# A new order of steps for both mixing stages of a two-layer hybrid decoder, with its engine and buffer tables

## The chip, the core and the metric

The kernel runs on one core of a Trainium2 chip. The metric is the device time of one execution in microseconds (us). TensorE (PE) multiplies, VectorE (DVE), ScalarE (ACT) and GpSimd (POOL) work on tiles, SyncE (SP) issues the transfers. Each engine works through its own instructions in the order in which the program issued them, and waits where one needs a result that is not there.

## The reference, cut to what matters

Two layers, 512 tokens, width 1024, all float32. Each layer has a mixing stage and an MLP:

```python
for l in range(DEPTH):
    h = rms_norm(x, norm_mix_g[l])
    proj = h @ w_in[l]                     # 1024 -> 3328 columns
    p_att, p_conv, p_rwkv = jnp.split(proj, [3 * ATT_W, 3 * ATT_W + 3 * CONV_W], axis=-1)
    ...
    o_att = diff_attention(q, k, v, lam, subln_g[l], lambda_init)   # 6 heads, causal
    o_conv = short_conv(b_gate, c_gate, u, conv_w[l])
    o_rwkv = rwkv7_time_mix(p_rwkv, ...)                            # 6 heads, recurrent state
    mixed = jnp.concatenate([o_att, o_conv, o_rwkv], axis=-1)
    x = x + mixed @ w_out[l]
    h = rms_norm(x, norm_mlp_g[l])
    x = x + jnp.square(jax.nn.relu(h @ w_mlp_up[l])) @ w_mlp_down[l]
return rms_norm(x, final_norm_g)
```

## The kernel before

A float32 product is made of three passes on rounded operands: the weight's high part by the activation's high part, high by low, and low by high (`whi`, `wlo` and `ahi`, `alo`; in the trace `ahim`, `alom`). For this, each weight tile of 128 x 512 is loaded as `raw`, ScalarE casts it to `whi` (L687), and VectorE or GpSimd subtracts to get `wlo` (L699). The table `LO` says, by `x` or `y`, which of the two engines does each of a layer's subtractions; the nine of the three head groups of layer 0 stay on VectorE.

A mixing stage has 26 groups of the input projection (`pj`), each 24 passes of 128*128 by 512 columns into one PSUM buffer, then eight groups of the output projection (`po0_...`; the rows called `po` with `pT` are attention's product with the values), each in two cuts, and the first three groups of the MLP's up projection. Beside these run the three pairs of attention heads (letters A, B, C), the two halves of the convolution (U, V), and three pairs of rwkv heads (R, S, T), each with a triangular inverse (r, s, t). Attention's score product is `sc`, its transposed probabilities `ptt`. Rwkv works in chunks of 64 tokens: `pg`, `pbv`, `pa`, `pst` (the state step) and others are its products. An inverse ends in four products that each need the one before, through a copy or an addition: `px`, `py`, `pz`, `pzz`, then `pzw` uses it. Between `px` and `py` stand two copies on ScalarE (`rt`, L1194).

All of this is written as Python generators, each of which yields one step at a time. `drive` takes steps from them as the string `ORDER[l]` says: a letter is one generator, a number behind it says how many steps. So the string fixes the order of instructions on every engine. The letters for the projections and their weights are d (loads), w (casts), x and y (subtractions on VectorE and GpSimd), m (projection passes) and o (additions of the output); n, g, h, i, p, N, e, q and k are norms, rates, gates, inputs, constants.

Buffers that exist several times are taken by the table `SLOTS`: for each pool and tag a digit for each tile in turn. `ps/mm` has two PSUM buffers for the projections, `ps/rp` four for the small products, `ps/at` two for attention, `wp/raw`, `wp/whi` and `wp/wlo` three each for the weights. A tile that takes a buffer waits until the former tile in it has been read. Copy-outs from projection buffers are the rows with `vf`, `kf` (L1294, L1267), `pg` and `pk` (L812).

The MLP and everything else are not driven by these tables. There the kernel has 32 up groups and the down product `dn`, whose result is added to `x` in L1537.

Of the kernel before, what the change touches and what calls it, by code (L numbers as in the profile page):

```python
# [22 lines left out]
S = 512  # L23
# [3 lines left out]
C = 64  # L27
# [24 lines left out]
LO = ("xxyyxxxxyxxyxyxyxyxyyxxxxyyxyyxxxyxyxyyyxxyxyyxxxxxyxxyyyxxyxyyyxxyxxyxxyyx",  # L52
      "xyxyyxxxxxyxxxxxxxxxxyxxyyyyyyxxyxxxxyyyyyyyxxxxyxxyyxyxyyxxyyxyxyyxyxxxxx")

ORDER = (
# [1571 lines left out]
```

## Time and profile before

| what | value |
|---|---|
| median of three runs | 1265.12 us (1264.98 to 1265.78) |
| the profiled execution's own time | 1265.12 us |
| its span | 1263.3 us |
| mixing stage of layer 0 (0 to 292 us) | TensorE busy 283.65 us |
| MLP of layer 0 (292 to 633 us) | TensorE busy 338.47 us |
| mixing stage of layer 1 (633 to 913 us) | TensorE busy 276.81 us |
| MLP of layer 1 and the end (913 to 1263.3 us) | TensorE busy 341.70 us |
| TensorE's granted clock in the four | 1.00, 1.00, 1.00, 0.99 |

A row of the timeline has the start in us, the duration, engine, line, operation, output and inputs, the part of the TensorE array used (128*128 is all of it), the shape and the count, and in brackets the idle time before with what ended it. The rows of one TensorE stage overlap, because passes are pipelined: the distance of two starts tells what a pass cost, the duration does not. The file is 17 lines shorter after the change, so L290 is L273 there, L687 is L670, L699 is L682, and so on.

### The profile page before, as it was taken

What the parts mean: (1) busy time and instruction counts of PE and PEld (TensorE: products, weight loads), DVE (VectorE), ACT (ScalarE), POOL (GpSimd) and SP (SyncE); (2) the same over time, 40 slices, a digit from 0 to 9 for tenths busy, and PEclk for the clock granted to TensorE, in tenths of its full rate; (3) what the DMA queues carried; (4) which work ended last, traced back from release to release, by engine and by line L of the source; (5) the groups of instructions that cost most, each with busy time, mean ns of one, the idle gap of its engine ahead of it and who ended that gap; (6) DMA issues with size and microseconds to landing.
All of it is one profiled execution on the core that took longest, in us unless ns stands there. A gap on an engine that the chain in (4) does not pass through costs nothing.

```text
span 1263.3 us, 25161 instructions
## 1 busy us (share of the span) xinstructions
PE 1240.6 (98%) x9493; PEld 1049.3 (83%) x9493; DVE 913.4 (72%) x1894; ACT 697.7 (55%) x1479; POOL 335.5 (27%) x434
## 2 busy tenths in 40 slices
PE   9999999999999999999999999999999999999997
PEld 6777777787789898989878887887787989898987
DVE  6788888867976666765667787879598766666654
ACT  7675655646744544544475656564575545454553
POOL 1343526133300101010224345352431010111110
PEclk9999999999999999999999999999999999999999
DMA  6533333142343333321235334331434233333122
GB/s 212 159 85 94 109 94 101 52 133 84 100 126 101 101 101 100 101 84 51 75 103 146 98 102 110 98 97 60 133 93 133 92 109 95 107 99 102 59 75 76
DMA packets 84698, 127.93 MB, mean 101 GB/s; under 512 B 21472, under 2 KB 25568, under 8 KB 84576
## 3 DMA queue, kind: packets, MB, share of 16 engines
q1 hardware_dynamic: 83856, 125.77, 32.4%
q8 instruction: 75, 1.23, 0.4%
q10 hardware_dynamic: 720, 0.55, 0.1%
q14 instruction: 47, 0.39, 0.1%
HBM read 117.11 MB, written 9.18 MB: 100 GB/s over the span
## 4 chain that ended last, share of the span: by engine, by line
PE 71%; DVE 3%; ACT 1%; issue 1%; POOL 0%; POOLq 0%; DVEq 0%; ACTq 0%
PE dn L290 22%; PE pj L290 11%; PE pa L290 11%; PE pb L290 6%; PE up L290 6%; PE po L290 4%; PE dnF L290 3%; PE pc L290 3%; PE sc L290 1%; PE ptt L295 1%; PE pg L290 1%; DVE wlo L344 0%; DVE blo L1461 0%; DVE x L1537 0%; PE pyy L290 0%
## 5 line engine op out<-in xcount | busy, mean ns | idle before, releaser
L1405 POOL TENSOR_TENSOR ml<-m,mh 128x512 fp32r<-128x512 f32 x64 | 95.2, 1490 | 509.0 <-ACT mh L1404 490.8
L343 ACT CAST whi<-raw 128x512 fp32r<-128x512 f32 x142 | 88.0, 621 | 173.9 <-PE dn L290 158.2
L290 PE MATMUL dn<-mh,whi 128*128 128x512 f32 x448 | 175.4, 391 | 2.0 <-DVE x L1537 2.0
L290 PE MATMUL dn<-mh,wlo 128*128 128x512 f32 x448 | 174.7, 390 | 0.0
L290 PE MATMUL dn<-ml,whi 128*128 128x512 f32 x448 | 174.6, 390 | 0.0
L290 PE MATMUL pj<-ahim,whi 128*128 128x512 f32 x392 | 157.6, 402 | 4.4 <-DVE vf L1294 1.8
L290 PE MATMUL pj<-ahim,wlo 128*128 128x512 f32 x392 | 158.3, 404 | 0.0
L290 PE MATMUL pj<-alom,whi 128*128 128x512 f32 x392 | 158.2, 404 | 0.0
L687 ACT CAST whi<-raw 128x512 fp32r<-128x512 f32 x142 | 87.6, 618 | 93.3 <-PE pj L290 40.6
L699 POOL TENSOR_TENSOR wlo<-raw,whi 128x512 fp32r<-128x512 f32 x62 | 81.7, 1317 | 215.3 <-ACT whi L687 199.1
L1537 DVE TENSOR_TENSOR x<-dn,x 128x512 f32<-128x512 f32 x112 | 76.8, 686 | 76.7 <-PE dn L290 76.7
L344 DVE TENSOR_TENSOR wlo<-raw,whi 128x512 fp32r<-128x512 f32 x142 | 115.2, 811 | 11.3 <-ACT whi L343 10.7
L1476 DVE TENSOR_TENSOR slo_p<-s,shi_p 128x512 fp32r<-128x512 f32 x96 | 70.9, 741 | 63.5 <-ACT shi_p L1475 58.8
L290 PEld LDWEIGHTS dn<-mh,whi 128*128 128x128 f32 x448 | 84.1, 188 | 21.5 <-issue 2.4
L290 PEld LDWEIGHTS dn<-mh,wlo 128*128 128x128 f32 x448 | 84.1, 188 | 17.9
L290 PEld LDWEIGHTS dn<-ml,whi 128*128 128x128 f32 x448 | 84.1, 188 | 16.5
L290 PEld LDWEIGHTS pj<-ahim,whi 128*128 128x128 f32 x392 | 73.9, 188 | 19.9 <-issue 1.7
L1475 ACT CAST shi_p<-s 128x512 fp32r<-128x512 f32 x96 | 59.2, 617 | 49.7 <-PE pa L290 38.1
L290 PEld LDWEIGHTS pj<-ahim,wlo 128*128 128x128 f32 x392 | 73.8, 188 | 14.3 <-issue 0.9
L290 PEld LDWEIGHTS pj<-alom,whi 128*128 128x128 f32 x392 | 73.9, 188 | 14.0 <-issue 0.5
L290 PE MATMUL pa<-tlo,shi_p 128*128 128x256 f32 x288 | 81.4, 282 | 0.0
L290 PE MATMUL pa<-thi,shi_p 128*128 128x256 f32 x288 | 81.2, 282 | 0.0
(417 smaller groups left out, 3255.3 us busy)
## 6 DMA issues: line engine op xcount, KB each, us to landing
raw<-wts SPq DMA_DIRECT2D x389, 256.0 KB, 2.7
qs<-dqhi SPq DMA_DIRECT2D x24, 128.0 KB, 3.2
ks<-dkhi SPq DMA_DIRECT2D x24, 128.0 KB, 3.8
x<-xT SPq DMA_DIRECT2D x8, 256.0 KB, 4.5
dqhi<-qhi SPq DMA_DIRECT2D x6, 256.0 KB, 3.4
dqlo<-qlo SPq DMA_DIRECT2D x6, 256.0 KB, 3.0
dkhi<-khi SPq DMA_DIRECT2D x6, 256.0 KB, 2.7
dklo<-klo SPq DMA_DIRECT2D x6, 256.0 KB, 3.1
```

Of the source, the lines that this page charges most:

```text
L290: ins = nc.tensor.matmul(*a, **k)
L295: ins = nc.tensor.transpose(*a, **k)
L343: act.copy(hi[:, :n], raw[:, :n])
L344: (pool if a and lean[0] else dve).tensor_tensor(lo[:, :n], raw[:, :n], hi[:, :n].bitcast(F32), ALU.subtract)
L687: yield act.copy(hi[:, k0:k1], raw[:, k0:k1])
L699: yield eng.tensor_tensor(lo[:, k0:k1], raw[:, k0:k1], hi[:, k0:k1].bitcast(F32), ALU.subtract)
L1405: pool.tensor_tensor(lo, m, hi.bitcast(F32), ALU.subtract)
L1475: act.copy(hi, src)
L1476: dve.tensor_tensor(lo, src, hi.bitcast(F32), ALU.subtract)
L1537: dve.tensor_tensor(x[j], pt, x[j], ALU.add)
```

## The change

Only three tables change: `LO`, `ORDER` and the entries of `SLOTS` that follow from the order. No function and no operation is added or removed, apart from what follows from the order (table loads on ScalarE, waits). In the diff's core a line or two of each:

```diff
-LO = ("xxyyxxxxyxxyxyxyxyxyyxxxxyyxyyxxxyxyxyyyxxyxyyxxxxxyxxyyyxxyxyyyxxyxxyxxyyx",
-      "xyxyyxxxxxyxxxxxxxxxxyxxyyyyyyxxyxxxxyyyyyyyxxxxyxxyyxyxyyxxyyxyxyyxyxxxxx")
+LO = ("xxxxxxyyyxyyyyxxyyyyxxxxyyxyyyyxxxxxyyyyyyyxyxxyyxyyxyyyyxyyxyxyyxxyxxxxyy",
+      "xyyxxyyyyyxyxyxyxyxyxxyyyyyxyyxxxxxxyyyyyyyyyxxxxxxyyyyyyyyyyyxyyxxxxxxxyx")
...
-         "m A r m A m A m2 A h m2 w S m2 A2 x m S h A m S A d m2 r m2 r2 m r m w m r2 m3 A m2 y m2 A r A m d S m r m r A m h w m r S A y B m r S B r d "
+         "S r S2 r h r2 R r3 m7 x m3 r2 A r m5 r2 m3 d m A2 r m2 A S2 m w A2 r2 A3 r A3 y m2 R d r S d2 m4 w y m S m A2 m4 w m2 w S2 m2 r S r3 x r5 "
...
-         "ps/mm 01010100101010101010110101010101010101010101 "
+         "ps/mm 10101011010101010101001010101010101010101010 "
...
-         "wp/wlo 01201201201201201201201201201201201201201201201201201201201201201201201201 ")
+         "wp/wlo 21021021021021021021202102102102120120120120120120120120120120120120120120 ")
```

Of the 151 subtractions of the two mixing stages, 89 are on VectorE and 62 on GpSimd before, 67 and 84 after. ScalarE's table loads are 11 before and 17 after. TensorE has the same 7785 matmuls; 777 of its instructions wait on another engine before, 855 after.

Two places show what moves. The first is on TensorE, in layer 1, in the inverse of the first rwkv pair: `px` is the product whose copies `rt` the product `py` needs, `pj` are projection passes (of groups 16 and 11), `pbv` belongs to the same rwkv pair, `ptt` and `po` to attention. Before:

```order
L290 MATMUL px1_0_1_8745<-yi1_0_8733,ee1_0_8731 64x64 x2
L290 MATMUL pj1_16_8678<-ahim1_7_7869,wlo114_4_8648 128x512
L290 MATMUL pj1_11_8770<-ahim1_0_7799,whi109_0_8676 128x512
L290 MATMUL pj1_11_8770<-alom1_0_7800,whi109_0_8676 128x512
L295 MATMUL ptt1_0_0_3_8778<-cst_77,pp1_0_0_3_0_8702 128x128 x4
L290 MATMUL py1_0_0_8789<-x16_1_0_8715,rt1_0_8768 64x64 x2
...
L290 MATMUL po1_0_0_8808<-v1_0_8436,pT1_0_0_8578 64x64 x20
L290 MATMUL pj1_11_8770<-ahim1_0_7799,wlo109_0_8684 128x512
```

And at the same place after:

```order
L273 MATMUL px1_0_1_8738<-yi1_0_8724,ee1_0_8722 64x64 x2
L273 MATMUL pbv1_0_0_8759<-vt1_0_8349,kq1_0_8224 64x64 x2
L273 MATMUL pbv1_0_1_8760<-vt1_0_8349,kq1_0_8224 64x64 x2
...
L273 MATMUL py1_0_0_8781<-x16_1_0_8700,rt1_0_8755 64x64 x2
L273 MATMUL py1_0_1_8782<-xs1_0_8702,rt1_0_8755 64x64 x2
...
L278 MATMUL ptt1_0_0_3_8801<-cst_77,pp1_0_0_3_0_8679 128x128 x4
L273 MATMUL pj1_11_8711<-ahim1_3_7811,wlo109_0_8686 128x512
L273 MATMUL pj1_11_8711<-ahim1_4_7815,whi109_4_8715 128x512
```

Between `px` and `py` stood three projection passes and four transposes; now there are sixteen small passes of `pbv` on the same tile size (the two rows alternate four times), and the projection passes come behind `py` in one run.

The second place is on TensorE in layer 0, where projection group 25 takes the PSUM buffer of group 6, which is copied out to `vf`. `sc` is attention's score product, `pvt` a transpose, `pa` and `pg` are rwkv products. Before:

```order
L290 MATMUL pj0_6_585<-alom0_7_260,whi6_4_538 128x512
L290 MATMUL pj0_6_585<-ahim0_7_259,wlo6_4_550 128x512
L290 MATMUL pj0_25_638<-ahim0_0_128,whi25_0_583 128x512
L295 MATMUL pvt0_0_641<-cst_77,vf0_0_634 128x128 x4
L290 MATMUL pj0_25_638<-alom0_0_129,whi25_0_583 128x512
```

And after:

```order
L273 MATMUL pj0_6_555<-ahim0_7_282,wlo6_4_571 128x512
L273 MATMUL pa0_1_616<-za0_366,lx160_398 128x512
...
L278 MATMUL pvt0_0_631<-cst_77,vf0_0_628 128x128 x4
L273 MATMUL pg0_0_0_0_640<-ar0_0_611,bk0_0_612 64x128
...
L273 MATMUL sc0_0_0_0_1_688<-ks0_0_0_624,qs0_0_0_530 128x128
L273 MATMUL pj0_25_704<-ahim0_0_128,whi25_0_588 128x512
```

Group 25's first pass directly followed group 6's last; now sixteen rows of other products stand between them.

More of the change, by code (lines that the diff above doesn't have):

```diff
@@ L50 @@
 OWN = (0, 5)
-LO = ("xxyyxxxxyxxyxyxyxyxyyxxxxyyxyyxxxyxyxyyyxxyxyyxxxxxyxxyyyxxyxyyyxxyxxyxxyyx",
-      "xyxyyxxxxxyxxxxxxxxxxyxxyyyyyyxxyxxxxyyyyyyyxxxxyxxyyxyxyyxxyyxyxyyxyxxxxx")
+LO = ("xxxxxxyyyxyyyyxxyyyyxxxxyyxyyyyxxxxxyyyyyyyxyxxyyxyyxyyyyxyyxyxyyxxyxxxxyy",
+      "xyyxxyyyyyxyxyxyxyxyxxyyyyyxyyxxxxxxyyyyyyyyyxxxxxxyyyyyyyyyyyyxyyxxxxxxyx")
 ORDER = (
[57 rows of a table removed]
[40 rows of a table added]
 SLOTS = (
@@ L116 @@
          "cp/ro 010 "
-         "cp/rr 01 "
-         "cp/rst 01201201 "
-         "cp/rsx 01201201 "
-         "cp/ry 010 "
-         "cp/ys 010 "
-         "dp/dkhi 010 "
-         "dp/dklo 010 "
-         "dp/dm 010 "
-         "dp/dn 010 "
-         "dp/dqhi 010 "
-         "dp/dqlo 010 "
-         "mp/av 012 "
-         "mp/dc 010 "
-         "mp/ks 101010 "
-         "mp/lw 012 "
-         "mp/mix 01201210 "
-         "mp/mx 012301230123012301230123012301230123012301230123 "
-         "mp/oss 010 "
-         "mp/pe1 01010010100 "
-         "mp/pp 011001100110011001100110011001100110011001100110 "
-         "mp/qs 101010 "
-         "mp/s0q 010 "
-         "mp/sm4 012301230123012301230123 "
-         "mp/ta 010101010 "
-         "mp/tc 010110 "
-         "mp/tp 01234510245234513512041025023524520013000341351302 "
-         "mp/tq 010101010101 "
-         "mp/ty 010101010 "
-         "ps/at 010101010101010101010101010101010101010101010101010101010101010101010101010101010101 "
-         "ps/mm 01011101010001010101010101010101010101010 "
-         "ps/rp 01233303103102310231023102310231023102021301230123012032121023102310202130123012301230123012013201313021032 "
-         "wp/raw 01201201201201201201201201201201201201201201201201201201201201201201201201 "
-         "wp/sq 010100001010101 "
-         "wp/whi 01201201201201201201201201201201201201201201201201201201201201201201 "
-         "wp/wlo 01201201201201201201201201201201201201201201201201201201201201201201 ",
-         "cp/rk 010 "
-         "cp/ro 010 "
-         "cp/rr 01 "
+         "cp/rr 10 "
          "cp/rst 01201201 "
@@ L168 @@
          "mp/lw 012 "
-         "mp/mix 01201021 "
+         "mp/mix 01201120 "
+         "mp/mx 012301230123012301230123012301230123012301230123 "
+         "mp/oss 010 "
+         "mp/pe1 01010010101 "
+         "mp/pp 011001100110011001100110011001100110011001100110 "
+         "mp/qs 010101 "
+         "mp/s0q 010 "
+         "mp/sm4 012301230123012301230123 "
+         "mp/ta 010101010 "
+         "mp/tc 010110 "
+         "mp/tp 01234510222245414132053021021254205131515431421452 "
+         "mp/tq 010101010101 "
+         "mp/ty 010101010 "
+         "ps/at 101010101010101010101010101010010101010101010101010101010110101010101010101010101010 "
+         "ps/mm 01011101010001010101010101010101010101010 "
+         "ps/rp 01233301203102302302031203201032103210102312031203210320132013012301212031023102312031203103103210303120132 "
+         "wp/raw 01201201201201201201201201201201201201201201201201201210210210210210210210 "
+         "wp/sq 101010110101010 "
+         "wp/whi 01201201201201201201201201201201201201201201201201201201201201201201 "
+         "wp/wlo 01201201201201201201201201201201201201201201201210210210210210210210 ",
+         "cp/rk 010 "
+         "cp/ro 010 "
+         "cp/rr 01 "
+         "cp/rst 01201210 "
+         "cp/rsx 01201210 "
+         "cp/ry 010 "
+         "cp/ys 010 "
+         "dp/dkhi 010 "
+         "dp/dklo 010 "
+         "dp/dm 010 "
+         "dp/dn 010 "
+         "dp/dqhi 010 "
+         "dp/dqlo 010 "
+         "mp/av 012 "
+         "mp/dc 010 "
+         "mp/ks 010101 "
+         "mp/lw 012 "
+         "mp/mix 01201020 "
          "mp/mx 012301230123012301230123012301230123012301230123 "
@@ L178 @@
          "mp/tc 010100 "
-         "mp/tp 01234510245235423143150241324125123504132413453420 "
+         "mp/tp 01234510245454535151403524152450451230415041021052 "
          "mp/tq 010101010101 "
@@ L182 @@
          "ps/at 010101010101010101010101010101010101010101010101010101010101010101010101010101010101 "
-         "ps/mm 01010100101010101010110101010101010101010101 "
-         "ps/rp 01230123012301230123012301231023102021301230123012301230123021032121302310231023013201320123012323102130 "
-         "wp/raw 01201201201201201201201201201201201201201201201201201201201201201201201201 "
-         "wp/sq 010101010 "
-         "wp/whi 01201201201201201201201201201201201201201201201201201201201201201201201201 "
-         "wp/wlo 01201201201201201201201201201201201201201201201201201201201201201201201201 ")
+         "ps/mm 10101011010101010101001010101010101010101010 "
+         "ps/rp 10321032103210321023102312301230123231021302130213021302130123012323102130213021321321012320132020312301 "
+         "wp/raw 12012012012012012101201201201210210210210210210210210210210210210210210210 "
+         "wp/sq 101010101 "
+         "wp/whi 21021021021021021021021021021021021021021021021021021021021021021021021021 "
+         "wp/wlo 21021021021021021202102102102120120120120120120120120120120120120120120120 ")
 NG = NG_IN + NG_OUT + NG_UP + NG_DN
```

96 rows, old and new, of the table ORDER are left out of this document.

## The prediction

> **What bounds the kernel now.** I read the page first, then the windows cut at the stage borders, then TensorE's waits, and last the timeline of TensorE at single places. The page's span, its first part and the first line of its chain of waits:
>
> ```profile
> span 1263.3 us, 25161 instructions
> PE 1240.6 (98%) x9493; PEld 1049.3 (83%) x9493; DVE 913.4 (72%) x1894; ACT 697.7 (55%) x1479; POOL 335.5 (27%) x434
> PE 71%; DVE 3%; ACT 1%; issue 1%; POOL 0%; POOLq 0%; DVEq 0%; ACTq 0%
> ```
>
> TensorE is busy for 98% of the span and idle for 1263.3 - 1240.6 = 22.7 us; no other engine comes to three quarters. So the reader should see two places where time can be had at all: those 22.7 us, and the way TensorE's own passes follow each other, since a "busy" matmul here includes what it loses at its start. The windows are the mixing stage of layer 0, its MLP, the mixing stage of layer 1, and its MLP with the end (columns: window, length, then busy time and count of PE, PEld, DVE, ACT, POOL, then granted clock, DMA share, GB/s):
>
> ```profile
> 0.00:292.00 292.00, 283.65 (x2740) 223.65 (x2740) 227.05 (x570) 178.10 (x417) 112.92 (x180) 1.00 0.38 114
> 292.00:633.00 341.00, 338.47 (x1964) 297.69 (x1964) 237.53 (x382) 174.06 (x326) 56.63 (x40) 1.00 0.30 94
> 633.00:913.00 280.00, 276.81 (x2731) 222.77 (x2730) 211.59 (x541) 166.44 (x396) 114.89 (x178) 1.00 0.35 105
> 913.00:1263.30 350.30, 341.70 (x2063) 305.22 (x2062) 237.23 (x405) 179.09 (x342) 51.06 (x36) 0.99 0.30 95
> ```
>
> The change touches the first and third window alone. Their idle time is 292.00 - 283.65 = 8.35 and 280.00 - 276.81 = 3.19 us: 11.5 us in all. A search that only removed waits could bring no more than that. Everything beyond must come from the spacing of passes, so I price that first.
>
> **Small tiles among the projections.** A projection pass (pj) is 128*128 with 512 columns. The rwkv and inverse steps are float32 passes on 64*64, 32*32 or 128*64 tiles. TensorE at such a place, in the timeline (start, duration):
>
> ```profile
> 159.45 0.40 PE L290 MATMUL pj<-ahim,wlo 128*128 128x512 f32 x1
> 159.69 0.39 PE L290 MATMUL pj<-ahim,whi 128*128 128x512 f32 x1
> 160.01 0.27 PE L290 MATMUL py<-x,rt 64*64 64x64 f32 x2
> ...
> 160.48 0.23 PE L290 MATMUL py<-xs,rt 64*64 64x64 f32 x2
> 160.63 0.50 PE L290 MATMUL pj<-alom,whi 128*128 128x512 f32 x1
> 160.97 0.40 PE L290 MATMUL pj<-ahim,wlo 128*128 128x512 f32 x1
> ...
> 713.23 0.23 PE L290 MATMUL py<-xs,rt 64*64 64x64 f32 x2
> 713.38 0.80 PE L290 MATMUL po<-v,pT 128*64 128x64 f32 x20
> ```
>
> Starts of projection passes lie 0.23 apart (the row after 159.45 says 0.24 by rounding). Going in takes 160.01 - 159.69 = 0.32, that is 0.09 more. Between py rows lie about 0.47 / 15 = 0.03; coming out takes 0.15, so 0.12 more, and the first pass after it 0.34, so 0.11 more: 0.23 together. Going from one small tile size to another (the last two rows) takes 0.15, where twenty po passes take 0.80, 0.04 each: 0.11 more.
>
> I counted the switches in the two orders (which the order gives exactly). Projections into small tiles: 57 before, 31 now. Small tiles back to the projections: 56, now 25. From small size to small size: 21, now 59. The sum is 26 x 0.09 + 31 x 0.23 - 38 x 0.11 = 2.3 + 7.1 - 4.2 = **5.3 us less**, all of it on TensorE's path, as nothing covers the pass that comes after a switch.
>
> [...] With one price for every change the three counts would be 134 and 115 and the gain smaller; that is a rival below.
>
> Two further shapes stay on the full tile. The state step of rwkv (pst):
>
> ```profile
> 111.41 0.48 PE L290 MATMUL pj<-ahim,whi 128*128 128x512 f32 x1
> 111.73 0.40 PE L290 MATMUL pj<-alom,whi 128*128 128x512 f32 x1
> 111.96 0.39 PE L290 MATMUL pj<-ahim,wlo 128*128 128x512 f32 x1
> 112.19 0.33 PE L290 MATMUL pst<-st,ad 128*128 128x64 f32 x2
> 112.33 0.48 PE L290 MATMUL pj<-ahim,whi 128*128 128x512 f32 x1
> ```
>
> It puts 0.14 between 112.19 and 112.33, and the pass after such a one starts 0.32 later (111.41 to 111.73): 0.14 + 0.32 - 0.23 = 0.23, of which its own work is part; I take half, 0.12. Returns of this kind fall from 35 to 23: 12 x 0.12 = **1.4 us less** (bounds 0 and 2.8). Attention scores on 96 rows (sc) between projections fall from 41 to 20. No row here has them alone; between nothing and 0.09, the cheapest entry above, I take 0.05: **1.0 us less** (bounds 0 and 1.9).
>
> **Accumulators that are not yet empty.** The projections use two PSUM buffers in turn; a group's first pass waits until the former group's result there has been copied out. TensorE's waits (total, times, longest), and one of them in the timeline:
>
> ```profile
> PE pj L290 <- DVE vf L1294: 1.8, 2, 0.9
> PE pj L290 <- DVE pg L812: 1.1, 1, 1.1
> PE pj L290 <- DVE pk L812: 0.7, 1, 0.7
> PE pj L290 <- DVE kf L1267: 0.4, 1, 0.4
> 53.14 0.39 PE L290 MATMUL pj<-ahim,wlo 128*128 128x512 f32 x1
> 54.41 0.47 PE L290 MATMUL pj<-ahim,whi 128*128 128x512 f32 x1 [0.88 <-DVE vf L1294]
> ```
>
> The second pass starts 1.27 after the first instead of 0.23. Four groups of before follow the former user of their buffer by 0.23 to 1.03 us of TensorE work (pj0_25 is the shortest). In the new order the shortest such distance inside the stages is 1.68 us, as other steps stand between; only layer 1's first group, pj1_24, has 0.23, behind the last down product. The four rows add to **4.0 us less** (bounds 2 and 4). For pj1_24 a copy-out is this row, and what may come back is the second:
>
> ```profile
> L1537 DVE TENSOR_TENSOR x<-dn,x 128x512 f32<-128x512 f32 x112 | 76.8, 686 | 76.7 <-PE dn L290 76.7
> PE pssm L290 <- DVE accm L455: 0.8, 1, 0.8
> ```
>
> It loses about 0.69 - 0.23 = 0.5; the later wait of pssm at that place then shrinks. I take **0.2 us more** (bounds -0.3 and 0.6).
>
> **The inverse's chain.** Six inverses have four steps each in which a product goes through a copy into the next product. In such a step the copies and TensorE looked like this before:
>
> ```profile
> 778.85 0.69 PE L290 MATMUL px<-yi,ee 64*64 64x64 f32 x32
> 779.48 0.50 PE L290 MATMUL pj<-ahim,whi 128*128 128x512 f32 x1
> 779.58 0.65 ACT L1194 COPY rt<-px 128x256 f32<-128x256 f32 x2 [0.23 <-PE px L290]
> 780.60 0.27 PE L290 MATMUL py<-x,rt 64*64 64x64 f32 x2
> ```
>
> The last px pass starts some 0.15 before 779.48, the copies end at 780.23: the step needs 0.9 us, and TensorE's projections covered 1.27. Before, these covers were 1.26 to 2.37 in all six. Now they are 0.25, 0.25, 0.63, 0.88, 1.43 and 1.49, since runs of small tiles stand together. The uncovered part is 0.65 + 0.65 + 0.27 + 0.02 = 1.6; the other three steps keep 0.78 to 5.12, which leaves some 0.4 open where the need is 0.9. So **2.0 us more** (bounds 0 and the slower rival below).
>
> Of the other waits I only know their number: 777 TensorE instructions waited on another engine, now 855. The 22.7 idle us over 777 are 0.03 each; 78 more give **2.3 us more** (bounds 0 and 4.6).
>
> **Work beside the path.** These rows are the low-part subtractions, a table load, the casts, and one vector operation beside a GpSimd operation (L407, at 628.25) and mostly without (L440):
>
> ```profile
> L699 POOL TENSOR_TENSOR wlo<-raw,whi 128x512 fp32r<-128x512 f32 x62 | 81.7, 1317 | 215.3 <-ACT whi L687 199.1 <-PE pj L290 7.7 <-DVE mlo L880 2.7
> L699 DVE TENSOR_TENSOR wlo<-raw,whi 128x512 fp32r<-128x512 f32 x80 | 56.3, 706 | 6.0 <-ACT whi L687 5.5
> L1333 ACT ACT_TABLE_LOAD x1 | 1.3, 1283 | 0.0
> L687 ACT CAST whi<-raw 128x512 fp32r<-128x512 f32 x142 | 87.6, 618 | 93.3 <-PE pj L290 40.6 <-PE po L290 24.8 <-issue 17.8
> L407 DVE SCALAR_TENSOR_TENSOR alom<-x,prm,ahim 128x512 fp32r<-128x512 f32 x6 | 7.4, 1240 | 4.5 <-ACT ahim L406 4.5
> L440 DVE SCALAR_TENSOR_TENSOR alom<-x,prm,ahim 128x512 fp32r<-128x512 f32 x10 | 7.3, 747 | 4.5 <-ACT ahim L439 4.5
> 627.74 1.29 POOL L400 TENSOR_TENSOR accm<-accm,sqm 128x512 f32<-128x512 f32 x1 [2.02 <-ACT sqm L394]
> 628.25 1.34 DVE L407 SCALAR_TENSOR_TENSOR alom<-x,prm,ahim 128x512 fp32r<-128x512 f32 x1 [0.78 <-ACT ahim L406]
> ```
>
> 22 subtractions go from VectorE to GpSimd: 22 x 0.706 = 15.5 us less on the one, 22 x 1.317 = 29.0 more on the other, whose two windows are 39% and 41% full. Table loads rise from 11 to 17: 6 x 1.283 = 7.7 us more on ScalarE, 61% full there. Weights wait two buffers ahead, so I set all this at nothing; the cover is the weight queue. If it is gone, a late subtraction costs 1.317 - 0.706 = 0.6 each, at most 13 us; a load that meets one of the chain's copies costs its 1.28, six of them 7.7.
>
> [...]
>
> **The sum.** -5.3 - 1.4 - 1.0 - 4.0 + 0.2 + 2.0 + 2.3 = -7.2 us. The profiled execution's own time is 1265.12 us, its span 1263.3 with 1.8 us around it, and it equals the median of the three runs. So 1265.1 - 7.2 = **1257.9 us**.
>
> **The rivals.** *One price for every switch.* A detour costs 0.09 + 0.23 = 0.32, or 0.16 for each of two switches; 134 to 115 switches would save 19 x 0.16 = 3.0, not 5.3, and the full-tile shapes nothing: -3.0 - 4.0 + 4.5 = -2.5, **1262.6 us**. For it: one mechanism. Against it: the 0.15 from py to po. Chance 0.15.
>
> [...] Each of the 22 GpSimd subtractions slows one vector operation beside it by 1.240 - 0.747 = 0.49: 10.8 of the 15.5 us are gone, evictions come no earlier, and the four waits stay somewhere: -5.3 - 2.4 + 4.5 + two of them more by 0.5 each = -2.2, **1262.9 us**, about the same. For it: the rows above. Against it: the waits came from distance in the order, not from a full VectorE. Chance 0.15.
>
> *Slower: the inverse's copies queue.* TensorE runs in order, so a step whose copy is late holds all projections behind it, and the copies stand on ScalarE among casts (0.62) and more table loads. With 24 steps each late by one cast, 0.62, plus the 1.6 uncovered: 16.5 in place of 2.0, so -7.2 + 14.5 = +7.3, **1272.4 us**. It decides from (7.2 + 2.0) / 24 = 0.38 us a step on. For it: six covers of px now below or near the need. Against it: the other steps have projections between. Chance 0.19; half as bad gives 1265.
>
> *The change does not do what it says.* The table loads rise by six in a search that counts them; should they lie on the path, 7.7 us cancel the gain: 1265.6, counted with the case of no change.
>
> The forecast has 0.48, and 0.03 is for a gain beyond the bounds. About 0.2%, 2.5 us, is what a measurement of this kernel can tell from no change. Faster by more than that: the forecast, the tail, and over half of the two middle cases, 0.67. The rest of these and of the mild late copies is within, 0.13; slower 0.20. The range goes from all bounds at their best, -5.3 - 2.8 - 1.9 - 4.0 - 0.3 = -14.3, about 1251, to the slower rival's middle, 1269.
>
> **What would show it.** In the changed kernel's windows PE busy should fall by some 5 us over the two mixing stages, the copy-out waits (vf, pg, pk, kf) should be gone from TensorE's waits, and py <- rt should appear among them with about 2 us. PE busy unchanged would make the switch prices wrong; py, pz and pzz with over 10 us of waits would make the slower rival right; waits of pj on wlo of L682 would show GpSimd short.

## The result, and the profile after

The changed kernel takes 1287.38 us (median of four runs, 1285.28 to 1288.8) against 1265.09 for the kernel before: a ratio of 1.0174, 95% interval 1.0156 to 1.0191. That is 22 us slower, where 7 us faster was forecast. The profiled execution has a span of 1285.7 us.

To see where the time went I cut both traces at the same five places of the program: the first plain projection pass with a `wlo` of its own, the first pass of `dn`, the first `pj` of layer 1, its first `dn`, and the end. So the stretch called a body, and layer 1's mixing stage too, reaches to the first `dn` and holds the first up groups of the MLP. The windows of before (window, length, then busy time and count of PE, PEld, DVE, ACT, POOL, then granted clock, DMA share, GB/s):

```profile
0.00:27.60 27.60, 24.64 (x101) 17.20 (x102) 18.13 (x43) 19.27 (x36) 2.68 (x8) 1.00 0.70 229
27.60:336.36 308.76, 301.87 (x2826) 240.56 (x2825) 246.60 (x594) 187.10 (x432) 122.97 (x182) 1.00 0.34 101
336.36:633.64 297.28, 295.93 (x1778) 263.62 (x1776) 200.34 (x315) 145.90 (x277) 43.91 (x32) 1.00 0.30 94
633.64:954.70 321.06, 318.19 (x2915) 257.00 (x2916) 249.10 (x607) 194.41 (x446) 126.23 (x184) 1.00 0.35 104
954.70:1263.30 308.60, 300.00 (x1877) 270.96 (x1875) 199.22 (x336) 151.01 (x292) 39.72 (x30) 0.99 0.30 94
```

And of the changed kernel:

```profile
0.00:44.73 44.73, 31.48 (x101) 22.12 (x102) 18.24 (x43) 19.58 (x36) 6.15 (x11) 0.81 0.47 148
44.73:351.70 306.97, 297.38 (x2827) 242.49 (x2825) 256.13 (x584) 190.75 (x440) 133.10 (x188) 1.00 0.34 101
351.70:648.18 296.48, 295.20 (x1778) 263.85 (x1776) 199.24 (x316) 144.89 (x274) 42.78 (x31) 1.00 0.30 93
648.18:975.52 327.34, 317.20 (x2916) 259.77 (x2916) 265.42 (x595) 192.75 (x447) 145.54 (x196) 0.99 0.34 103
975.52:1285.70 310.18, 300.90 (x1877) 271.41 (x1875) 199.16 (x337) 151.39 (x293) 39.76 (x30) 0.99 0.30 94
```

Three things are to be seen. The **opening** does the same 101 instructions of TensorE in 44.73 us instead of 27.60: 17.1 us, the bulk of the loss. The **body of layer 0** is 1.8 us shorter: TensorE is busy 4.5 us less, and idle 9.59 instead of 6.89. **Layer 1's mixing stage** is 6.3 us longer: busy 1.0 us less, but idle 10.14 instead of 2.87. So the spacing did improve; the waits grew by more. The end is 1.6 us longer and the MLP of layer 0 is 0.8 shorter.

In the opening TensorE waits, and is then slow. Here `pj` stands for passes of the three head groups, whose weights are `whi_s` and `wlo_s`; an input tile's two roundings `ahim` and `alom` are called its entry. The changed kernel's windows around its waits, and the first of these in the timeline:

```profile
8.00:12.30 4.30, 0.68 (x4) 0.21 (x2) 1.99 (x4) 3.43 (x6) 0.00 (x0) 1.00 0.11 40
12.30:16.30 4.00, 4.00 (x11) 3.13 (x12) 3.51 (x6) 0.96 (x3) 0.00 (x0) 0.57 0.64 197
...
33.50:40.40 6.90, 6.82 (x25) 6.11 (x26) 1.05 (x7) 0.26 (x2) 0.00 (x0) 0.52 0.11 37
12.28 0.50 PE L273 MATMUL pj<-ahim,wlo_s 128*128 128x512 f32 x1 [3.62 <-DVE wlo_s L682]
12.84 0.62 PE L273 MATMUL pj<-alom,whi_s 128*128 128x512 f32 x1
13.26 0.63 PE L273 MATMUL pj<-ahim,wlo_s 128*128 128x512 f32 x1
```

After 3.62 us of waiting the passes start 0.42 apart (12.84 to 13.26) instead of 0.23, until about 16.25, 3.4 us later; the mean granted clock of the window is 0.57. The other waits of the opening are these:

```profile
22.79 0.57 PE L273 MATMUL pj<-alom,whi_s 128*128 128x512 f32 x1 [2.22 <-DVE alom L423]
28.93 0.50 PE L273 MATMUL pj<-ahim,whi_s 128*128 128x512 f32 x1 [2.59 <-ACT ahim L422]
33.58 1.86 PE L273 MATMUL pssm<-ones,accm 128*128 128x1 f32 x8 [2.88 <-DVE accm L438]
```

Their causes stand on the other engines. VectorE, ScalarE, GpSimd and SyncE of the changed kernel:

```profile
9.90 0.75 DVE L423 SCALAR_TENSOR_TENSOR alom<-x,prm,ahim 128x512 fp32r<-128x512 f32 x1 [2.24 <-ACT ahim L422]
11.67 1.49 DVE L682 TENSOR_TENSOR wlo_s<-raw,whi_s 128x384 fp32r<-128x384 f32 x3
27.33 0.62 ACT L670 CAST whi<-raw 128x512 fp32r<-128x512 f32 x1 [6.27 <-DMA raw<-wts]
28.16 1.33 ACT L422 ACTIVATE ahim<-x,prm 128x512 fp32r<-128x512 f32 x2
12.29 1.30 SPq L630 DMA_DIRECT2D raw<-wts  x3
13.64 1.86 SPq L634 DMA_DIRECT2D x<-xT  x4
23.13 9.59 SPq L630 DMA_DIRECT2D raw<-wts  x5
30.59 1.78 POOL L682 TENSOR_TENSOR wlo<-raw,whi 128x512 fp32r<-128x512 f32 x1 [1.30 <-ACT whi L670]
31.24 1.68 DVE L423 SCALAR_TENSOR_TENSOR alom<-x,prm,ahim 128x512 fp32r<-128x512 f32 x1
```

And SyncE of the kernel before, at its second group of loads:

```profile
7.38 2.44 SPq L647 DMA_DIRECT2D raw<-wts  x3
```

The subtractions `wlo_s` of 128x384 stand on VectorE behind an entry (`alom`) that waits 2.24 us for its input; until they are done, their `raw` buffers are not free, and SyncE's next loads, at 7.38 before, go at 12.29 (that the one holds the other is tested below). Later ScalarE stands 6.27 us at a cast of a plain weight tile whose load SyncE issues only at 23.13, and the casts of the inputs (`ahim`) queue behind it. The last `alom` takes 1.68 us beside a GpSimd subtraction, where the one at 9.90 takes 0.75, so by these rows some 0.9 of the 2.88 us for the sum is a collision of these two engines and not a step in the wrong place.

In the bodies, TensorE's waits on attention's `pp` and `ot` and on the inverse grew. Of the changed kernel, by total, times and longest:

```profile
PE ptt L278 <- DVE pp L1322: 4.2, 7, 1.2
PE pot L278 <- DVE ot L1347: 2.3, 2, 1.5
PE px L273 <- DVE yi L1169: 2.1, 2, 1.3
PE px L273 <- DVE sm L1318: 1.4, 1, 1.4
```

The kernel before has only the first of these in its list:

```profile
PE ptt L295 <- DVE pp L1339: 2.8, 4, 0.9
```

One of the longest waits of layer 1, with VectorE, GpSimd and TensorE of the changed kernel in its neighbourhood:

```profile
723.18 2.84 DVE L1158 TENSOR_TENSOR xs<-xd,cst 64x256 f32<-64x256 f32 x2
726.05 0.71 DVE L1169 STREAM_TRANSPOSE yi<-x 128x512 f32<-128x512 f32 x1
722.56 1.75 POOL L1167 TENSOR_TENSOR ee<-nn,cst 128x512 f32<-128x512 f32 x1
724.43 2.72 POOL L682 TENSOR_TENSOR wlo<-raw,whi 128x512 fp32r<-128x512 f32 x2
726.91 0.70 PE L273 MATMUL px<-yi,ee 64*64 64x64 f32 x32 [1.37 <-DVE sm L1318]
```

The product px needs `yi`, which ends at 726.76; the profile names `sm`, the operation behind it. Ahead of `yi` two operations `xs`, also steps of the inverse, take 2.84 us; by the groups of lines such a one took 0.420 on average before (twelve of them) and 0.834 now, before and after in turn:

```profile
L1175 DVE TENSOR_TENSOR xs<-xd,cst 64x256 f32<-64x256 f32 x12 | 5.0, 420 | 0.3
```

```profile
L1158 DVE TENSOR_TENSOR xs<-xd,cst 64x256 f32<-64x256 f32 x12 | 10.0, 834 | 0.2
L682 POOL TENSOR_TENSOR wlo<-raw,whi 128x512 fp32r<-128x512 f32 x84 | 114.0, 1361 | 194.2 <-ACT whi L670 174.0 <-PE po L273 7.6 <-DVE rst L369 5.0
```

The 0.834 is a mean of two kinds: five of the twelve took 1.40 to 1.43 us, each beside a GpSimd operation, and seven took 0.42, none beside one. Each of the two above begins while a GpSimd operation runs and ends about 0.3 us after it: the first at 724.59, behind `ee`'s end at 724.30, the second at 726.02, behind the end of the first `wlo` at 725.74. I summed this over a mixing stage: what each VectorE operation took, less the shortest of its kind in the two traces. That excess is 22.6 us in layer 0 and 18.3 in layer 1 before, 32.9 and 38.8 after; the sums move by some us with the ends of the stretch, and all of the growth lies in operations that ran beside a GpSimd operation. So 15.5 us of subtractions left VectorE, and about 31 us of lengthening of its other operations came.

### The profile page after: what moved, and what is told of

It is laid out like the page before. It is cut to its first block, busy times and chain, and to the rows that moved or that the text cites. A ratio compares the mean times of both kernels' runs of the same rounds, so it can differ in the third digit from the quotient of the medians.

```text
span 1285.7 us, 25139 instructions
## 1 busy us (share of the span) xinstructions
PE 1242.2 (97%) x9493; PEld 1059.6 (82%) x9493; DVE 938.2 (73%) x1872; ACT 699.4 (54%) x1485; POOL 367.3 (29%) x456
## 4 chain that ended last, share of the span: by engine, by line
PE 77%; DVE 13%; ACT 3%; DMA 2%; issue 2%; POOL 1%; SPq 0%; POOLq 0%; DVEq 0%; ACTq 0%
PE dn L273 22%; PE pj L273 15%; PE pa L273 11%; PE po L273 7%; PE pb L273 5%; PE dnF L273 3%; PE up L273 3%; PE pc L273 3%; PE sc L273 1%; PE ptt L278 1%; DMA raw<-wts 1%; DVE wlo L327 1%; DMA x<-xT 1%; DVE sm L1320 1%; DVE xs L1158 1%
## 5 line engine op out<-in xcount | busy, mean ns | idle before, releaser
L682 POOL TENSOR_TENSOR wlo<-raw,whi 128x512 fp32r<-128x512 f32 x84 | 114.0, 1361 | 194.2 <-ACT whi L670 174.0
L273 PE MATMUL pj<-alom,whi 128*128 128x512 f32 x392 | 155.1, 396 | 0.0
```

Source lines behind the costliest of these rows:

```text
L273: ins = nc.tensor.matmul(*a, **k)
L682: yield eng.tensor_tensor(lo[:, k0:k1], raw[:, k0:k1], hi[:, k0:k1].bitcast(F32), ALU.subtract)
```

## The experiments

Each ratio is against runs of the kernel before on the same chip. Versions that ran on different chips are compared by their ratios, times 1265 us, and not by their medians. Line numbers differ from version to version.

**Three subtractions early.** In the changed order:

```diff
-m x2 m3 q e w3 e4 q3 x3 e q2 m2 q
+m x2 m3 q e w3 x3 e4 q3 e q2 m2 q
```

> The changed order with one edit: the three 128x384 subtractions of the head groups stand directly behind their casts, ahead of two entry steps and three squares, instead of behind them. Theory A (one late step starts the whole loss of the opening): TensorE's 3.6 us wait at the second head pass goes, SyncE's next weight loads start near 8 us instead of 12.3, the inputs x4 to x7 come 4 us earlier and the three later waits of 2.2, 2.6 and 2.9 us shrink to a third: 1271 to 1277 us. Rival B (each wait of the opening has its own place in the order): only the first wait and the slow passes behind it go, 3.6 + 1.6 = 5 us: about 1282 us.

Measured 1282.97 us (1.0148, 1.0127 to 1.0169): 3.3 us back, and in the traces the opening is 3.9 us shorter, ending at 40.85. The wait on `wlo_s` is gone, though 1.56 us on `alom` stands near its place. SyncE's loads go at 7.63 instead of 12.29, so these subtractions did hold them, but the later waits stay: 2.2 us on `alom`, 3.5 on `ahim`, 2.9 on the sum. Theory A falls, rival B stands: one late step did not make the rest.

**The same three late in the kernel before.** The segment `m q m2 w m x e m w e m x m w d m3 x d e m3 d2 e q m3` became:

```diff
+q w e w e w d d e d2 e q x3 m16
```

> The kernel before with one edit: the same three 128x384 subtractions moved late, behind two entry steps. Theory A: a wait of TensorE of about 3.6 us, a lower granted clock behind it, weight loads and inputs 4 us later: 1275 to 1282 us. Rival B: the wait and its slow passes alone, about 1270 us.

Measured 1268.58 us (1.0024, 1.0015 to 1.0033), 3.1 us more. TensorE's wait on `wlo_s` is 1.5 us there, and one on `ahim` 1.9; SyncE's loads go at 10.49 instead of 7.38, and the opening ends at 31.10, 3.5 later. So the step costs about 3 us in both orders. Rival B's 1270 us is near; theory A's far larger loss did not come, though its chain is there in small: later loads, and a wait on inputs behind them.

**Casts behind the entries.** On top of the first edit, casts of plain weight tiles (w) were moved on ScalarE. First one cast went behind three more entry casts and two squares, to the place where the second already stood; then both went behind all entries:

```diff
-d6 w d k4 e3 m e m5 k2 q2 w m4 e m3 k e2 m2 q m n2
+d7 k4 e3 m e m5 k2 q2 w2 m4 e m3 k e2 m2 q m n2
```

> As the run with the three subtractions early, and the cast of the first plain weight tile moved behind three entry casts and two squares on ScalarE. Theory F (that cast waits on ScalarE for a weight load which comes late, and holds the inputs' casts behind it): TensorE's waits on ahim (3.5 us) and on accm (2.9 us) go, with the slow passes behind them: 1283 - 7 = about 1276 us. Rival G (the inputs themselves or the squares' buffers are late): within 2 us of 1283 us.

```diff
-d7 k4 e3 m e m5 k2 q2 w2 m4 e m3 k e2 m2 q m n2
+d7 k4 e3 m e m5 k2 q2 m4 e m3 k e2 m2 q m w2 n2
```

> As the run with the casts moved behind three entries, but now both casts of plain weight tiles stand behind all eight entries and the squares. In that run TensorE waited 6.3 us for the sum of squares, whose last square came behind an entry that stood behind these casts on ScalarE, and the casts waited 2.1 us for a weight load. Theory F (the casts ahead of the entries): that wait falls to under 1.5 us and the passes behind it are no longer slow: 1281.7 - 6 = about 1276 us or less. Rival G (inputs and squares are late by themselves): the wait stays above 4 us, 1280 us or more.

The first measured 1281.74 us (1.0124, 1.011 to 1.0138), within 2 us of 1283 as rival G had it; by the ratios it is 3.0 less, with intervals that overlap. Its trace does not fit rival G, and so the second was run: 1275.2 us (1.0083, 1.0065 to 1.0102), by the ratios another 5.2 us less, as theory F had it; the opening ends at 34.44 instead of 38.91. TensorE's wait for the norm's sum of squares, with the casts half way:

```profile
27.60 1.87 PE L167 MATMUL pssm<-ones,accm 128*128 128x1 f32 x8 [6.32 <-DVE accm L332]
```

And with them last:

```profile
23.48 1.86 PE L167 MATMUL pssm<-ones,accm 128*128 128x1 f32 x8 [2.23 <-DVE accm L332]
```

Half way, the waits had only moved from the inputs to the sum, since the last entry, and behind it VectorE's last addition to the sum (`accm`), still came after the casts. With the casts last, 2.2 us are left where theory F had said under 1.5.

**The constants' cast.** One more cast that waited for its load was moved behind two entries:

```diff
-d7 k4 e3 m e m5 k2 q2
+d7 e3 m e m5 k6 q2
```

> As the run with both casts last, and the cast of the exact constants, which waited 2.4 us on ScalarE for its load, moved behind two entries. Theory F (any cast that waits for a load ahead of the entries holds TensorE): the wait on alom of 1.7 us goes, with the slow passes behind it: 1272 to 1273.5 us. Rival G: 1275 us as without it.

Measured 1274.36 us (1.0069, 1.0054 to 1.0085), 1.8 less by the ratios, with intervals that overlap; its opening is not shorter (34.86), and the wait on `alom` stayed, 2.0 us. This cast does not hold it. So of the opening's 17.1 us these single steps account for 10.3 (44.73 to 34.44). The last 6.8, of which 4.1 are idle time and 2.7 slower passes, are not traced to single steps.

**The opening of before as a whole.** The first 139 steps of before, then the new order; and the first 178, to the end of the first norm:

> The changed kernel with the opening steps of the kernel before (its first 139 steps, up to the end of entry and squares; the two buffers of the squares as there), then the new order. The head should reach its first plain projection pass near 27 us instead of 44.3. Theory A and rival B alike: 17 us less, about 1270 us, so that the rest of the new order is still about 5 us slower than before. Rival C (the rest of the new order gains its 7 us once the opening is as before): 1258 us.

> The changed kernel with the steps of the kernel before until the first norm's last step (178 steps instead of 139), then the new order with its own engines for the subtractions. Theory B (each wait of the opening has its own place; in the run with 139 steps the norm's own steps still stood too close, 2.6 us of wait and slow passes): the first plain projection pass comes near 28 us, and 1274.4 - 5 = about 1269.5 us. Rival A2 (the opening's remaining 5 us come from the weight loads behind it): no better than 1273 us.

Measured 1274.41 us (1.0075, 1.006 to 1.009) and 1269.76 us (1.003, 1.0018 to 1.0041): by the ratios 12.5 and 18.2 us back, so that the opening is shown to be the bulk of the loss. Theory B had the second right; rival C, by which the rest would then gain its 7 us, falls. With 139 steps, where 1270 us had been expected, my cut left one pass between the norm's sum and its broadcast, so that one of these numbers is partly the cut's own:

```profile
25.79 1.96 PE L167 MATMUL prbm<-cst,rrm 128*128 128x128 f32 x8 [2.56 <-issue]
```

With 178 steps the opening ends at 29.09 in this trace, and at 27.87 to 28.34 in the six other versions below that share it. Against before on the same chip 3.7 us remain, most of them behind the opening.

**Layer by layer.** The changed kernel with layer 1 as before, and the version with 178 steps with layer 1 as before:

> The changed kernel with the tables of the kernel before for layer 1. Theory D (layer 1 loses by waits on VectorE, 11 us more, against 4.6 us gained in spacing and some slow passes): 1287.4 - 8 = about 1279 us. Rival E (all of the loss is layer 0's, layer 1 gains its 4.6 us): about 1291 us.

> The same, and layer 1's tables as before: only the body of layer 0's mixing stage is new. By the stages of the runs so far the body of layer 0 is 0 to 2 us shorter: 1263 to 1266 us. If the forecast's spacing gain of some 4 us in that layer were not eaten by waits: 1261 us.

Measured 1283.54 us (1.0144, 1.0127 to 1.0161) and 1265.96 us (1.0002, 0.9992 to 1.0011): both times layer 1's new tables cost 3.8 us. Theory D holds at half its size, and rival E falls. The new body of layer 0 comes out even: the second version is level with before.

**Where the subtractions run.** Theory P has layer 1 lose because VectorE's operations take longer beside a GpSimd subtraction, as the second `xs` above did (1.42 us, where 0.42 is usual), and because `yi`, `ot` and `pp` come late by that. The version with 178 steps, all of layer 1's subtractions on VectorE: by theory P the excess there falls from 37 to under 20 us, and the mixing stage is 3 to 5 us shorter. The kernel before with the new engine table alone: by theory P 10 us more of excess a layer, and 1267 to 1271 us.

```diff
-LO[1]: 43 y and 31 x       (order of steps kept, y written as x)
+LO[1]: 74 x
```

> As the run with 178 steps, but in layer 1 all 43 subtractions of GpSimd go to VectorE; the order of steps stays. [...] Rival Q (VectorE is too full at these places, and 43 x 0.7 = 30 us more work make it worse): 3 us longer or more.

> The kernel before with the new table of engines alone: the same order of steps, 22 subtractions moved from VectorE to GpSimd as in the change. [...] Rival Q (VectorE's load counts, and 15.5 us less of it help): 1262 to 1265 us.

The first measured 1276.19 us (1.0078, 1.0063 to 1.0093), 6.4 us slower than with 178 steps. Theory P was nearly right on the excess, which fell from about 38 to about 22 us, and wrong on the time. TensorE now waits for subtractions, which come late in VectorE's queue, 7 us in all:

```profile
PE pj L167 <- DVE wlo L576: 5.5, 4, 2.5
...
PE po L167 <- DVE wlo L576: 1.8, 2, 0.9
```

The second measured 1271.97 us (1.0047, 1.0032 to 1.0062), about 6 us slower than before, with no step moved: theory P's side, just above its range, though the excess grew by about 3 and 5 us in the two layers rather than 10 each. 15.5 us less of VectorE's own work did not help. Nor were GpSimd's subtractions late themselves: no wait of TensorE on one of them stands in that trace, while its waits on VectorE's results grew (on `accm` from 0.8 to 2.1 us, and a new one of 1.6 on `zv`). So a table that does well with one order does badly with another, and neither engine is simply too full.

**Single collisions.** In the trace with 178 steps I took the GpSimd subtractions that ran beside a lengthened VectorE operation just ahead of a long wait of TensorE, and gave these alone to VectorE, at their places: eight in layer 1; five more in layer 0; and the five with layer 1 as before. By theory P the five waits that the eight stood ahead of, 1.4, 0.6, 0.9, 1.3 and 0.3 us, lose most of their length: 3 us less, about 1267 us.

```diff
-LO[1][23, 24, 25, 42, 43, 53, 59, 60] = y
+LO[1][23, 24, 25, 42, 43, 53, 59, 60] = x
```

> As the run with 178 steps, but in layer 1 only the eight GpSimd subtractions that ran beside a lengthened VectorE operation just ahead of one of TensorE's longest waits go to VectorE, at the same places of the order. [...] Rival Q (VectorE is simply late there, and 8 x 0.7 us more work does not help): 1270 us or more, with waits on wlo in their place.

> The same, and five such subtractions of layer 0 too. Theory P: waits of 1.4, 1.1, 0.9, 0.8 and 0.5 us there lose most of their length: another 3 us, about 1264 us. Rival Q: 1270 us or more.

> The run with 178 steps and layer 1 as before, and the five subtractions of layer 0 on VectorE: the one version of these that could beat the kernel before. Theory P: 1266 - 3 = about 1263 us, the gain in spacing less a few waits. Rival Q: 1266 us or more.

Measured 1266.55 us (1.0011, 1.0002 to 1.002), 1264.94 us (0.9991, 0.9982 to 1.0) and **1260.9 us (0.9964, 0.9951 to 0.9976)**: 2.4, another 1.6, and 4.8 us less than without. The middle one cannot be told from before. In the traces the edited stage itself gives a smaller number: layer 1's goes from 323.68 to 322.16 us with the eight, layer 0's body from 307.95 to 305.33 with the five. The rest lies in stages that the edit did not touch, and the second and third versions, which differ in layer 1's tables alone and ran on one chip, are still 4.0 us apart. So theory P holds for single collisions, at some 1.5 and 2.6 us; the eight did not make up for layer 1's loss, and not all five of its waits shrank. In the first of these the two `xs` of the place above take 1.83 us instead of 2.84; one GpSimd operation (`ee`) is still beside them, and px waits 0.4 at that place:

```profile
706.34 1.83 DVE L1052 TENSOR_TENSOR xs<-xd,cst 64x256 f32<-64x256 f32 x2
```

The third is the only version whose interval lies clear below the kernel before: before's opening, the new body of layer 0 with five subtractions moved back, before's layer 1. Its body of layer 0:

```profile
28.24:333.57 305.33, 297.59 (x2826) 242.79 (x2825) 255.11 (x592) 191.17 (x440) 127.49 (x185) 1.00 0.34 102
```

TensorE is busy 4.3 us less than in before's row and idle 7.74 instead of 6.89. Here the gain in spacing is kept.

**Five more in layer 1:**

> As the run with thirteen subtractions on VectorE, and five more of layer 1 that ran beside a lengthened VectorE operation or ahead of a wait. Theory P: 1 to 2 us less, 1263 to 1264 us. Rival Q (VectorE is now full enough that the moved ones come late themselves): 1265 us or more, with waits of TensorE on wlo.

Measured 1265.18 us (0.9993, 0.9984 to 1.0001), the same as with thirteen. By the number that is rival Q's side, but no wait on `wlo` stood out, so its reason was not seen; in the trace the edited stage is 1.5 us shorter and the end, which was not edited, 1.5 longer. This run decides nothing. In the trace with eight moved, the twelve `xs` still took 0.666 us on average, where it was 0.420 before.

## Why the prediction was wrong, step by step

**Spacing, -7.7 us: right.** TensorE's busy time fell by 4.5 us in layer 0's body. In layer 1 it fell by 1.0 in the changed kernel, where a clock of 0.64 after one wait lengthened some passes, and by 3.0 in the version with 178 steps. Together 7.5; in the changed kernel alone 5.5. The row of layer 1 in that version:

```profile
635.18:958.86 323.68, 315.17 (x2915) 258.42 (x2916) 264.30 (x595) 192.96 (x447) 145.88 (x196) 1.00 0.34 104
```

Busy time is not spacing alone: with all of layer 1's subtractions on VectorE and the same order of steps it is 318.17 us, and in layer 0 the version with 178 steps is only 1.4 us below before, with a mean granted clock of 0.99 there, where before has 1.00. Still, the rival with one price for every switch, 3.0, falls. The price of a change between two small sizes was not tested by itself.

**Accumulators not yet empty, -4.0 us: right.** No wait of TensorE on `vf`, `pg`, `pk` or `kf` is left in the changed kernel. **Layer 1's start, +0.2: right.** Its first pass waits 0.9 us on `x` instead of 0.3, and the later wait of pssm there, 0.8 before, is gone.

**The inverse's chain, +2.0 us, and the slower rival: wrong place.** The shortened covers cost 0.3 us at py:

```profile
PE py L273 <- ACT rt L1177: 0.3, 1, 0.3
```

The inverse does wait, 2.1 + 1.4 us, but ahead of px, for VectorE's `yi`, one step before the chain that I measured. That the 2.0 us of this term comes near these waits is luck. The slower rival's 1272.4 us was nearer to the measured time than the forecast, but for another reason: the copies did not queue.

**Other waits, +2.3 us by count: the failed step.** I priced 78 more waiting instructions at the mean of 0.03 us, and never read the order's opening engine by engine, although the first 30 us were in the order and in the trace. There steps stand in the queues of VectorE and ScalarE behind others that wait for loads, and TensorE's waits were 3.6, 2.2, 2.6 and 2.9 us. In place of 2.3 us the runs showed 10.3 us of idle time and 6.8 us of slower passes in the opening alone; before's opening, put back whole, gave 18.2 us back. Idle time in the two bodies grew by 2.7 and 7.3 us, which the next term shares.

**Work beside the path, 0 us: the second step that failed.** I set it at nothing because weights wait two buffers ahead. Their queue was not the way on which it reached TensorE. The rival in which each GpSimd subtraction slows one vector operation beside it had this, at 0.49 us a collision and 10.8 in all, and ended "about the same" because I let it fall only on evictions. Measured were about 31 us of excess, 1.0 for each of the two `xs` above. It fell on what stood next in VectorE's queue, here `xs`, and through `yi` and px on TensorE; the new engine table alone, with before's order, cost 5.9 us. The two `xs` took 1.42 us each, where 0.420 is usual, and both ended about 0.3 us after a GpSimd operation. My 0.49 from L407 against L440 was the price of one kind of place: five of the six L407 rows stood beside a GpSimd operation, but they began about 0.5 us after it (628.25 against 627.74), with 0.8 us of it left, and took 0.59 us longer than L440's mean. The two `xs` above began with 1.1 us left of theirs, and took 1.0 longer, twice my 0.49. So in these rows more was lost where more of the GpSimd operation was left; why VectorE's operations take longer there, no run shows.

The table loads, six more, are no part of any wait that I found, and the fastest version still has 15 of them against 11 before; no run moved them alone, so that they cost nothing is not shown.

## What to carry to other kernels

Walk a new order from its first instruction, on every engine's queue at once, and ask of each step that waits for a load what is queued behind it and which buffers it keeps: in the opening nothing has run ahead yet, and three subtractions and two casts in the wrong place cost 10.3 us there, more than all the gain in spacing. A table of engines belongs to its order; change the two together, and look for collisions one by one, on the operations just ahead of TensorE's longest waits.

## What the runs showed of the hardware that I had not expected

In the changed kernel's opening a wait of TensorE cost more than itself: after 3.62 us of it, passes stood 0.42 us apart instead of 0.23 for about 3.4 us, at a mean granted clock of 0.57 from 12.30 to 16.30. In its layer 1 there was no full stop: TensorE was busy for 1.38 of 3.20 us, 43%, and in the window behind it the mean granted clock was 0.64.

```profile
900.00:903.20 3.20, 1.38 (x8) 0.67 (x7) 3.09 (x7) 0.62 (x1) 1.26 (x1) 1.00 0.22 82
903.20:908.00 4.80, 4.78 (x16) 3.88 (x17) 3.78 (x6) 1.93 (x3) 0.00 (x0) 0.64 0.18 58
```

The trace has the granted clock at half from 903.7 to 907.1, 3.4 us, about as long as the slow stretch of the opening. How little work is enough for the clock to fall, no run shows.
